# FFN splits, convolution and forms on 1024 columns at once, three of seven products added in PSUM, weight sums from GpSimd to VectorE

## The chip, the cores and the metric

The kernel runs on one core of one Trainium2 chip. The metric is the device time of one execution in microseconds. The core's engines are named as in the profile: PE (TensorE, matrix products), DVE (VectorE), ACT (ScalarE), POOL (GpSimd), and SP (SyncE, which issues the DMAs). SBUF is the core's memory of 128 partitions, PSUM the eight accumulator banks that PE writes; a bank holds 512 fp32 numbers per partition.

## The reference

A decoder trunk in fp32 on one sequence of 1024 tokens and 1024 channels: an mLSTM layer and a convolution (conformer) layer, each followed by a gated feed-forward block with a short convolution, which is what the change is mostly about.

```
def conv_ffn(h, w_up, conv_w, conv_b, w_down):        # h: 1024 tokens x 1024
    u = causal_dwconv(h @ w_up, conv_w, conv_b)       # 1024 x 5632, 3 taps along the tokens
    gate, val = jnp.split(u, 2, axis=-1)              # 2816 each
    return (jax.nn.silu(gate) * val) @ w_down         # 2816 -> 1024

for layer in range(2):
    # six modulation vectors from c (a vector times a 1024 x 6144 matrix, "ada")
    x = x + g1 * mixer(modulate(rmsnorm(x)))          # layer 0 mLSTM (inner width 2048), layer 1 conformer
    x = x + g2 * conv_ffn(modulate(rmsnorm(x)))
return rmsnorm(x)
```

The mLSTM multiplies the normed input by a 1024 x 4096 matrix; the second half of the result is `z`, whose SiLU gates the output.

## The kernel before

Channels lie on the partitions, tokens along the free dimension: 1024 columns (`S`), taken as two halves of 512 (`HS`).

**Products in fp32.** An operand is split into a rounded part and a rest: `split` writes the rounded part with a cast on ACT (L174) and the rest with a subtraction on DVE, or on POOL where `engine` says so (L175). A block of 128 x 128 weights times 512 columns then takes three matmuls (`PASS`).

**Seven products for eight.** In z, in the FFN's up product and in its down product, blocks of the weights and halves of the activations form a 2 x 2 product, which is done with seven multiplications instead of eight. `Forms` prepares the seven left operands from two raw tiles of weights of 128 x 1024 (`raw`, one DMA of 512 KB each): `early` splits a11 and a12, `sums` makes s1, s3, s2 and s4 out of the raw tiles with four additions and subtractions on POOL (L511 to L514), and `late` splits the other five. The right operands b11, b21, t1 to t4, b22 are made once for all pairs. `Seven.product(q)` runs product q: `HALF` = 4 blocks of three matmuls, 12 in all, into a bank of its own; a pair takes 84. The products come in the order 0 to 6.

**The FFN's up product (`ffn_up`).** It loops over 22 pairs j: block j of the gate channels (g) and block j of the value channels (FB + j). Pairs 0 to 2 (`LEAD`) are interleaved with the norm and with the making of the right operands (the start, below); from pair 3 on each pair runs its seven products in turn (the steady pairs). Behind a product its bank is drained into the tiles `u`: `keep` and `tail` copy products 0 and 2 on ACT, and `join` (L633) and `tail` (L718 to L726) make the four results c11, c12, c21, c22 with seven additions on DVE. `conv` makes each half of 512 columns: ACT starts it with a scaled copy (L699), DVE adds two taps (L702). ACT takes the SiLU of the gate's half (L729), POOL multiplies it by the value's half (L730), and SP writes the half to the tensor `p_d` in HBM.

**The passage to the down product.** During the last up pair the operands of the down product are read back from `p_d` (`raw<-p_d`), combined (L573) and split into tiles `h` (L175); the first down step's products 0 to 3 (L807) run as their operands come. `ffn_down` then takes steps m of 84 matmuls; its results are added into x, scaled by the modulation's gate, by `residual` (L457), eight per step.

**z.** The same seven products over eight pairs, with ten blocks of the ada product (L157) on DVE in between; here POOL splits the weights of pairs 2 to 7.

**Order.** A scheduler fixes each engine's order when the kernel is built, from the order and the priorities of the code; on the chip each engine takes its instructions strictly in that order and waits on semaphores. Tiles come out of rings of `bufs` buffers: the tag `wu` has six tiles of 512 columns, `wx` two; a tile is written again when its last reader is done.

Of the kernel before, what the change touches and what calls it, by code (L numbers as in the profile page):

```python
# [79 lines left out]
def trunk(ctx, tc, a):  # L80
# [96 lines left out]
    def load_weight(src, tag="wu", pool=wpool, bufs=6, ahead=30, engine=None, take=None):  # L177
        with tc.high_priority(ahead):
            r = raw_tile()
            n = src.shape[-1] // 2  # L180
            dma(r[:, : 2 * n], src)
            w = []
            for i in range(2):
                t = take() if take else pool.tile([P, 2, 512], F32R, tag=tag, name=nm(tag), bufs=bufs)
# [274 lines left out]
    def ring(*parts):  # L459
        slots = [(pool, tag, n) for pool, tag, n in parts for _ in range(n)]  # L460
        at = [0]

        def take():
            pool, tag, n = slots[at[0] % len(slots)]
            at[0] += 1
            return pool.tile([P, 2, HS], F32R, tag=tag, name=nm(tag), bufs=n)

        return take

    def chain_products(o, w, acts, n, first, last):  # L470
        for k in range(n):
            for q, (i, j) in enumerate(PASS):
# [5 lines left out]
                    stop=last and k == n - 1 and q == 2,  # L478
                )

    class Forms:
        """The seven left operands of the 2 x 2 product with seven multiplications."""

        def __init__(self, g, val, take, engine=None):
            self.src, self.take, self.engine = (g, val), take, engine
            self.raw = [None, None]
            self.rest = None
# [6 lines left out]

        def form(self, name, src):
            t = self.take()
# [10 lines left out]
        def sums(self):  # L507
            a11, a12 = self.load(0)
            a21, a22 = self.load(1)
            s1 = t512()  # L510
            gp.tensor_tensor(s1, a21, a22, ALU.add)  # L511
            gp.tensor_tensor(a21, a11, a21, ALU.subtract)
            gp.tensor_tensor(a11, s1, a11, ALU.subtract)  # L513
            gp.tensor_tensor(a12, a12, a11, ALU.subtract)  # L514
            self.rest = [("s1", s1), ("s3", a21), ("s2", a11), ("s4", a12), ("a22", a22)]

        def late(self, n=5, i=0):
            if self.rest is None:
                self.sums()
            for _ in range(n):  # L520
                self.form(*self.rest.pop(i))

    PRODUCTS = (("a11", "b11"), ("a12", "b21"), ("s1", "t1"), ("s3", "t3"), ("s2", "t2"), ("s4", "b22"), ("a22", "t4"))

    class Seven:
        """C = A B in seven products."""

        def __init__(self, forms, right, n):
            self.forms, self.right, self.n = forms, right, n
            self.banks = [None] * 7  # L530

        def product(self, q):
# [71 lines left out]
    def ffn_up(layer, normed, p_d, hx, ux, es_u, other, ops):  # L604
        first = ring((wpool, "wu", 6))
        pairs = {}

        def pair(j, take):
            pairs[j] = Forms(a["fup"][layer, j], a["fup"][layer, FB + j], take)
            pairs[j].early(j >= LEAD)  # L610
            if 0 < j < 3:
                pairs[j].engine = gp

        LEAD = 3
        for j in range(LEAD):
            pair(j, first)
# [8 lines left out]
        def part(b, h):  # L625
            return u[b][:, FK - 1 + h * HS : FK - 1 + (h + 1) * HS]

        def keep(j, s):
            channel(j)
            sc.copy(part(j, 1), s.banks[0])  # L630
# [1297 lines left out]
```

## Time and profile before

| | |
|---|---|
| median of three runs | 2857.96 us (2856.01 to 2861.04) |
| the profiled execution, first to last instruction | 2862.4 us |
| busy: PE, DVE, ACT, POOL | 2582.8, 2536.0, 1353.0, 1046.6 us |
| granted PE clock over the span | 0.948 of full speed |

The page gives no other time of the profiled execution than its span. By the page's slices the stages are: the mLSTM's up stream to about 290 us; z to 490; attention to 760; the mLSTM's down product to 940; the first FFN's up product to 1400 and its down product to 1600; the conformer to 2130; the second FFN to 2760; the last norm. A busy share is an average over stages with different limits; a busy PE is not PE at its peak, since matmuls are pipelined and their rate follows the granted clock. A row of `windows` gives, for a stretch of time, each engine's busy time with its number of instructions. A row of the timeline gives start, duration and, in brackets, how long the engine had stood idle before it and what released it.

### The profile page before, as it was taken

The page shows a single profiled execution, that of the slowest core. Times are in us where ns is not written, and L with a number is a line of the kernel's source. Part 1 is how long each engine was busy: PE and PEld are TensorE (multiplying, and loading weights), DVE is VectorE, ACT ScalarE, POOL GpSimd, SP SyncE. Part 2 cuts the span into 40 slices and gives each one's busy share as a digit, 9 for nine tenths or more (in the row PEclk, how much of TensorE's full clock was granted, in tenths as well). Part 3 has the DMA queues.
Part 4 walks back from the last instruction along what each step waited for, and adds up shares of the span by engine and source line. Part 5 has one row for each costly group of instructions (what it writes and reads, how often), then busy time and mean ns, then how long its engine had stood idle before and what let it go on. Part 6 is the DMA issues. An engine that isn't in the chain of part 4 may idle for free. (4 is left out here: it accounts for less than half of the span.)

```text
span 2862.4 us, 33276 instructions
## 1 busy us (share of the span) xinstructions
PE 2582.8 (90%) x11405; PEld 2076.4 (73%) x11405; DVE 2536.0 (89%) x3346; ACT 1353.0 (47%) x2422; POOL 1046.6 (37%) x814
## 2 busy tenths in 40 slices
PE   4899798999999899999798998868798999997998
PEld 2788676888788677777576887756576777774777
DVE  7999988777877999999999679996989999999986
ACT  4655334776635444444434342247554444444434
POOL 5312576332100555454432013443225554544220
PEclk7999899999999999999899999988899999997999
DMA  7576357532685222222242331111432222224222
GB/s 264 169 252 221 109 192 239 167 104 67 210 280 185 75 96 74 81 74 82 81 147 94 113 114 46 45 37 31 146 103 67 94 76 81 74 82 151 92 83 94
DMA packets 138392, 342.92 MB, mean 120 GB/s; under 512 B 13872, under 2 KB 36080, under 8 KB 138224
## 3 DMA queue, kind: packets, MB, share of 16 engines
q1 hardware_dynamic: 138224, 340.81, 36.0%
q8 instruction: 90, 1.47, 0.2%
q14 instruction: 78, 0.64, 0.1%
HBM read 264.18 MB, written 73.43 MB: 118 GB/s over the span
## 5 line engine op out<-in xcount | busy, mean ns | idle before, releaser
L473 PE MATMUL ps<-h,wu 128*128 128x512 f32 x4368 | 1065.4, 401 | 71.7 <-DVE wu L175 30.4
L473 PEld LDWEIGHTS ps<-h,wu 128*128 128x128 f32 x4368 | 833.6, 193 | 287.9 <-DVE wu L175 44.6
L195 PE MATMUL ps<-h,wu 128*128 128x512 f32 (+1 forms) x2478 | 585.4, 393 | 17.6 <-DVE h L175 12.0
L195 PEld LDWEIGHTS ps<-h,wu 128*128 128x128 f32 x2478 | 463.1, 191 | 122.2 <-DVE h L175 14.8
L175 DVE TENSOR_TENSOR wu<-raw,wu 128x512 fp32r<-128x512 f32 (+1 forms) x418 | 361.3, 871 | 57.7 <-ACT wu L174 57.1
L702 DVE SCALAR_TENSOR_TENSOR c<-u,par,c 128x512 f32<-128x512 f32 x352 | 374.5, 1091 | 11.9 <-ACT c L699 10.8
L174 ACT CAST wu<-raw 128x512 fp32r<-128x512 f32 (+1 forms) x484 | 288.0, 613 | 188.6 <-PE ps L195 63.9
L511 POOL TENSOR_TENSOR t<-raw 128x512 f32<-128x512 f32 x68 | 108.3, 1593 | 651.1 <-DMA raw<-in_fup 356.6
L699 ACT ACTIVATE c<-u,par 128x512 f32<-128x512 f32 x176 | 138.9, 813 | 372.9 <-DVE u L633 173.0
L473 PE MATMUL ps<-h,wx 128*128 128x512 f32 x1152 | 281.9, 397 | 10.1 <-DVE wx L175 6.7
L473 PEld LDWEIGHTS ps<-h,wx 128*128 128x128 f32 x1152 | 216.2, 188 | 65.7 <-DVE wx L175 10.2
L1680 DVE SCALAR_TENSOR_TENSOR cy<-cu,par,cy 128x512 f32<-128x512 f32 x180 | 179.0, 1031 | 4.6 <-ACT cy L1670 2.7
L730 POOL TENSOR_TENSOR c<-c,c 128x512 f32<-128x512 f32 x88 | 148.5, 1703 | 93.6 <-DVE c L702 88.5
L175 DVE TENSOR_TENSOR h<-raw,h 128x512 fp32r<-128x512 f32 (+1 forms) x204 | 160.7, 817 | 24.2 <-ACT h L174 23.9
L174 ACT CAST h<-raw 128x512 fp32r<-128x512 f32 (+1 forms) x204 | 117.4, 607 | 106.2 <-DVE raw L573 39.9
L157 DVE SCALAR_TENSOR_TENSOR ada<-ada,crep 128x1024 f32<-128x1024 f32 x96 | 126.4, 1320 | 27.0 <-DMA ada<-in_ada 26.8
L175 POOL TENSOR_TENSOR wu<-raw,wu 128x512 fp32r<-128x512 f32 x66 | 107.2, 1640 | 89.3 <-ACT wu L174 89.2
L457 DVE SCALAR_TENSOR_TENSOR x<-ps,mod,x 128x512 f32<-128x512 f32 (+1 forms) x152 | 106.7, 717 | 30.2 <-PE ps L195 23.9
L513 POOL TENSOR_TENSOR raw<-t,raw 128x512 f32<-128x512 f32 x68 | 111.2, 1635 | 36.7 <-DVE wu L175 25.0
L1330 PE MATMUL ps<-q,h 128*128 128x512 f32 (+2 forms) x576 | 117.1, 352 | 1.5 <-ACT q L174 1.3
L1367 PE MATMUL ps<-pt,vr 128*128 128x512 f32 (+2 forms) x576 | 116.2, 351 | 2.4 <-ACT pt L174 1.6
L514 POOL TENSOR_TENSOR raw<-raw 128x512 f32<-128x512 f32 x68 | 111.7, 1643 | 7.8 <-DVE wu L175 3.2
(282 smaller groups left out, 3855.8 us busy)
## 6 DMA issues: line engine op xcount, KB each, us to landing
ada<-in_ada SPq DMA_DIRECT2D x96, 512.0 KB, 4.3
raw<-in_fup SPq DMA_DIRECT2D x94, 512.0 KB, 3.6
p_d<-c SPq DMA_DIRECT2D x88, 256.0 KB, 2.0
raw<-in_pw SPq DMA_DIRECT2D x36, 512.0 KB, 3.6
raw<-in_mup SPq DMA_DIRECT2D x33, 512.0 KB, 4.6
raw<-p_d SPq DMA_DIRECT2D x32, 512.0 KB, 3.3
raw<-in_fdownS SPq DMA_DIRECT2D x32, 512.0 KB, 3.6
raw<-in_mdown SPq DMA_DIRECT2D x24, 512.0 KB, 4.1
```

What stands on the lines that cost most here:

```text
L157: v.scalar_tensor_tensor(w, w, 1.0, crep, ALU.mult, ALU.mult, accum_out=mod[:, layer, b : b + 1])
L174: sc.copy(out_hi, raw)
L175: (engine or v).tensor_tensor(out_lo, raw, out_hi.bitcast(F32), ALU.subtract)
L195: pe.matmul(o, t[:, i, c : c + P], acts[k][:, j, :], start=k == 0 and n == 0, stop=k == nk - 1 and n == 2,)
L473: pe.matmul(o, w[:, i, k * P : (k + 1) * P], acts[k][:, j, :], start=first and k == 0 and q == 0, stop=last and k == n - 1 and q == 2,)
L514: gp.tensor_tensor(a12, a12, a11, ALU.subtract)
L699: sc.activation(c, part(b, h), AF.Identity, scale=taps[FK - 1], bias=pv("fcb", layer, b))
L702: v.scalar_tensor_tensor(c, u[b][:, i + c0 : i + c0 + HS], taps[i], c, ALU.mult, ALU.add)
L730: gp.tensor_tensor(c, s.gates[h], c, ALU.mult)
L1330: pe.matmul(so[:, tlo:], xr[cc][I // nJ][:, i, I % nJ * P : (I % nJ + 1) * P], un["qs"][cc][:, j, tlo:], start=n == 0, stop=n == 3 * CB - 1,)
L1367: pe.matmul(un["num"][cc][:, tlo:], vr[I][:, i, cc * P : (cc + 1) * P], pt[:, j, tlo:], start=I == 0 and n == 0, stop=I == nJ * (hf + 1) - ...
L1680: v.scalar_tensor_tensor(y, u[:, t + c0 : t + c0 + HS], pv("dww", t, j), y, ALU.mult, ALU.add)
```

## The change

- **One instruction for two.** `split` of a raw tile, the FFN's convolution, its SiLU, the gate product and the write of `p_d` work on 1024 columns. Split tiles are `double` tiles of [128, 2, 1024], three in the ring in place of six; s1, which stands alone, gets a single tile (tag `w1`, two buffers, or a slot of the ring of raw tiles).
- **Three products add in PSUM.** Products 1, 5 and 6 accumulate onto the banks of 0, 2 and 3 (`ONTO`), in the order 0, 3, 2, 1, 6, 4, 5. The values of the banks that are overwritten in this way are taken out before: `combine` copies product 0 and product 2 on ACT and adds product 3 on DVE (L573 of the changed kernel). A pair of the up product then has five additions on DVE (L573 to L585) and, with c11, three copies on ACT; a step of the down product has six residuals.
- **From POOL to DVE.** The four sums of a pair (now L522 to L525), the splits of pairs 1 and 2 and of the first down step, and the gate product (now L701). POOL keeps, of this work, the splits of z's pairs 2 to 7, 1024 columns wide.
- The calls of `late` move with it: s1 and raw tile 1 (s3 and a22) are split behind product 6 of the pair before, raw tile 0 (s2 and s4) behind the first product of the pair itself.

DVE in a steady up pair, before: the end of one pair, from the addition of product 5 (L723) on. c are the convolution's tiles, u the results, wu and wx split weights.

```order
L723 TENSOR_TENSOR u_10353<-u_10353,ps_10450 128x512
L175 TENSOR_TENSOR wu_10447<-raw_10377,wu_10447 128x512
L702 SCALAR_TENSOR_TENSOR c_10464<-u_10353,par,c_10464 128x512
L726 TENSOR_TENSOR u_10397<-u_10397,ps_10468 128x512
L702 SCALAR_TENSOR_TENSOR c_10464<-u_10353,par,c_10464 128x512
L175 TENSOR_TENSOR wx_10527<-raw_10525,wx_10527 128x512
L702 SCALAR_TENSOR_TENSOR c_10482<-u_10397,par,c_10482 128x512
L702 SCALAR_TENSOR_TENSOR c_10489<-u_10397,par,c_10489 128x512
L702 SCALAR_TENSOR_TENSOR c_10482<-u_10397,par,c_10482 128x512
L702 SCALAR_TENSOR_TENSOR c_10489<-u_10397,par,c_10489 128x512
L175 TENSOR_TENSOR wx_10530<-raw_10525,wx_10530 128x512
L633 TENSOR_TENSOR u_10509<-u_10509,ps_10512 128x512
```

Products of the pair are drained and its taps follow in halves, up to the next pair's first addition (L633). The same place in the changed kernel, from the addition of product 5 (L585) to the next pair's L573, which empties product 3's bank (w is s1's tile, t its sum):

```order
L585 TENSOR_TENSOR u_8837<-u_8837,ps_8853 128x512
L773 SCALAR_TENSOR_TENSOR c_8929<-u_8866,par,c_8929 128x1024
L175 TENSOR_TENSOR wu_8966<-raw_8883,wu_8966 128x1024
L773 SCALAR_TENSOR_TENSOR c_8929<-u_8866,par,c_8929 128x1024
L773 SCALAR_TENSOR_TENSOR c_8946<-u_8837,par,c_8946 128x1024
L522 TENSOR_TENSOR t_1395_9034<-raw_9020 128x512
L773 SCALAR_TENSOR_TENSOR c_8946<-u_8837,par,c_8946 128x1024
L523 TENSOR_TENSOR raw_9020<-raw_9015,raw_9020 128x512
L175 TENSOR_TENSOR w_1396_9039<-t_1395_9034,w_1396_9039 128x512
L701 TENSOR_TENSOR c_8946<-c_8946,c_8929 128x1024
L573 TENSOR_TENSOR u_8998<-u_8998,ps_8972 128x512
```

The taps (L702, now L773) and the gate product stand together ahead of L573, with the sums between them.

POOL in the passage to the down product, before, from the last up pair's sums on (raw_11511 and raw_11519 are the first down step's weights):

```order
L175 TENSOR_TENSOR wu_11513<-raw_11511,wu_11513 128x512
L511 TENSOR_TENSOR t_1887_11580<-raw_11519 128x512
L512 TENSOR_TENSOR raw_11519<-raw_11511,raw_11519 128x512
L513 TENSOR_TENSOR raw_11511<-t_1887_11580,raw_11511 128x512
L730 TENSOR_TENSOR c_11418<-c_11329,c_11418 128x512
L175 TENSOR_TENSOR wu_11516<-raw_11511,wu_11516 128x512
L514 TENSOR_TENSOR raw_11511<-raw_11511 128x512
L730 TENSOR_TENSOR c_11425<-c_11400,c_11425 128x512
L175 TENSOR_TENSOR wu_11585<-t_1887_11580,wu_11585 128x512
```

and in the changed kernel POOL's last instructions of this FFN and the first of the conformer (L1619):

```order
L675 MEMSET u_10450 128x2
L675 MEMSET u_10553 128x2
L675 MEMSET u_10685 128x2
L675 MEMSET u_10743 128x2
L1619 MEMSET u_1898_12748 128x8x8
```

Sums, splits and gate products have gone to DVE; the zeroing of the two columns ahead of a convolution's tile is left.

PE in a steady up pair, before: products 0 and 1, each four blocks of three matmuls, each with a bank `ps` of its own.

```order
L473 MATMUL ps_8780<-h_7724,wu_8655 128x512 x3
L473 MATMUL ps_8780<-h_7729,wu_8655 128x512 x3
L473 MATMUL ps_8780<-h_7772,wu_8655 128x512 x3
L473 MATMUL ps_8780<-h_7777,wu_8655 128x512 x3
L473 MATMUL ps_8796<-h_7820,wu_8658 128x512 x3
L473 MATMUL ps_8796<-h_7825,wu_8658 128x512 x3
L473 MATMUL ps_8796<-h_7868,wu_8658 128x512 x3
L473 MATMUL ps_8796<-h_7873,wu_8658 128x512 x3
```

And changed: products 2, 1 and 6 of a pair.

```order
L470 MATMUL ps_8721<-h_7891,w_1351_8643 128x512 x3
L470 MATMUL ps_8721<-h_7897,w_1351_8643 128x512 x3
L470 MATMUL ps_8721<-h_7903,w_1351_8643 128x512 x3
L470 MATMUL ps_8721<-h_7909,w_1351_8643 128x512 x3
L470 MATMUL ps_8689<-h_7582,wu_8621 128x512 x3
L470 MATMUL ps_8689<-h_7587,wu_8621 128x512 x3
L470 MATMUL ps_8689<-h_7627,wu_8621 128x512 x3
L470 MATMUL ps_8689<-h_7632,wu_8621 128x512 x3
L470 MATMUL ps_8708<-h_8012,wu_8646 128x512 x3
L470 MATMUL ps_8708<-h_8016,wu_8646 128x512 x3
L470 MATMUL ps_8708<-h_8020,wu_8646 128x512 x3
L470 MATMUL ps_8708<-h_8024,wu_8646 128x512 x3
```

ps_8689 is the bank of product 0 and ps_8708 that of product 3: products 1 and 6 now come behind and add onto them.

The diff, cut to what matters (the calls in z and the start follow the same pattern):

```diff
+    def double(pool=wpool, tag="wu", bufs=3):
+        return pool.tile([P, 2, 2 * HS], F32R, tag=tag, name=nm(tag), bufs=bufs)
...
     class Forms:
+        LATE = ("s1", "raw1", "raw0")
+        def two(self, i, left, right):
+            self.load(i)
+            t = double()
+            split(self.raw[i], t[:, 0], t[:, 1], self.engine)
+            setattr(self, left, t[:, :, :HS])
+            setattr(self, right, t[:, :, HS:])
         def early(self, keep=True):
-            a11, a12 = self.load(0)
-            self.form("a11", a11)
-            self.form("a12", a12)
+            self.two(0, "a11", "a12")
...
-            gp.tensor_tensor(s1, a21, a22, ALU.add)
-            gp.tensor_tensor(a21, a11, a21, ALU.subtract)
-            gp.tensor_tensor(a11, s1, a11, ALU.subtract)
-            gp.tensor_tensor(a12, a12, a11, ALU.subtract)
+            v.tensor_tensor(s1, a21, a22, ALU.add)
+            v.tensor_tensor(a21, a11, a21, ALU.subtract)
+            v.tensor_tensor(a11, s1, a11, ALU.subtract)
+            v.tensor_tensor(a12, a12, a11, ALU.subtract)
...
+    ORDER = (0, 3, 2, 1, 6, 4, 5)
+    ONTO = {1: 0, 5: 2, 6: 3}
     class Seven:
         def product(self, q):
             w, b = PRODUCTS[q]
-            o = self.banks[q] = ps()
-            chain_products(o, getattr(self.forms, w), self.right[b], self.n, True, True)
+            if q in ONTO:
+                self.banks[q] = self.banks[ONTO[q]]
+            else:
+                self.banks[q] = ps()
+            chain_products(self.banks[q], getattr(self.forms, w), self.right[b], self.n, q not in ONTO, True)
+        def combine(self, q, top, bottom, ready):
+            o, done = self.banks, self.done
+            done.add(q)
+            halves = lambda t: (t[:, :HS], t[:, HS:])
+            if q == 0:
+                sc.copy(halves(top())[1], o[0])
+            elif q == 1:
+                ready("c11", o[1])
+            elif q == 2:
+                sc.copy(halves(bottom())[1], o[2])
+            if q in (2, 3) and {2, 3} <= done:
+                c22 = halves(bottom())[1]
+                v.tensor_tensor(c22, c22, o[3], ALU.add)
+            if q == 4:
+                c12, (c21, c22) = halves(top())[1], halves(bottom())
+                self.at = c12 if 6 in done else c21
+                v.tensor_tensor(self.at, c12, o[4], ALU.add)
+                v.tensor_tensor(c22, c22, self.at, ALU.add)
+                ready("c22", c22)
+                if 6 in done:
+                    v.tensor_tensor(c21, c12, o[6], ALU.add)
+                    ready("c21", c21)
+            if (q in (4, 5)) and {4, 5} <= done:
+                c12 = halves(top())[1]
+                v.tensor_tensor(c12, self.at, o[5], ALU.add)
+                ready("c12", c12)
...
     def ffn_up(layer, normed, p_d, hx, ux, es_u, other, ops):
-            if 0 < j < 3:
-                pairs[j].engine = gp
...
+            def ready(name, at):
+                if name == "c11":
+                    sc.copy(top()[:, :HS], at)
+                s.ready.add(name)
+                if name in ("c11", "c12") and {"c11", "c12"} <= s.ready:
+                    s.gate = conv(j)
+                    sc.activation(s.gate, s.gate, AF.Silu)
+                elif name in ("c21", "c22") and {"c21", "c22"} <= s.ready:
+                    s.val = conv(FB + j)
+                if len(s.ready) == 4:
+                    v.tensor_tensor(s.gate, s.gate, s.val, ALU.mult)
+                    dma(p_d[j], s.gate)
...
-            c = rx.tile([P, HS], F32, tag="c", name=nm("c"), bufs=5)
+            c = rx.tile([P, S], F32, tag="c", name=nm("c"), bufs=2)
...
-                    gp.tensor_tensor(c, s.gates[h], c, ALU.mult)
-                    dma(p_d[j][:, h * HS : (h + 1) * HS], c)
...
-                    if q == 2:
-                        down = down_forms(layer, 0, 0, ring((wpool, "wu", 6)), gp)
+                    if q == 1:
+                        down = down_forms(layer, 0, 0, single(wpool, "raw", 3))
```

More of the change, by code (lines that the diff above doesn't have):

```diff
@@ L678, in ffn_up @@
         group(0)
-        pairs[0].late(2)
-        pairs[1].late(1)
+        pairs[0].late("raw1")
+        pairs[1].late("s1")
         group(1)
-        for j, s in enumerate(seven):
-            join(j, s)
         both = seven[:2]
@@ L734, in ffn_up @@
-        for q in range(4, 7):
-            pairs[1].late(1)
-            if q == 6:
-                pairs[2].take = more
-                pairs[2].late()
-            for j, s in enumerate(both):
+        for j, s in enumerate(both):
+            for q in (2, 3):
+                evacuate(j, s, q)
+        pairs[1].one = pairs[2].one = more
+        pairs[1].late("s2", "s4")
+        for j, s in enumerate(both):
+            for q in range(4, 7):
                 s.product(q)
-                if q == 4:
-                    tail(j, s, 2)
-                tail(j, s, q)
+                evacuate(j, s, q)
+                if (j, q) == (1, 5):
+                    pairs[2].late("s1", "raw1")
@@ L744, in ffn_up @@
+        pairs[2].late("raw0")
         for name in ops.FORMS:
@@ L781, in ffn_down @@
             ops.extra, ops.bufs = dx, 1
-            take = ring((dx, "wx", 2), (wpool, "wu", 6))
+            one = single(dx, "w1", 2)
             acts = [[], []]
@@ L816, in ffn_down @@
                         s = Seven(forms, right, CHUNK // 2)
-                    kt = []
-                    for q in range(7):
-                        if m or q > 3:
+                    o = s.banks
+                    for n, q in enumerate(ORDER if m else (0, 1, 2, 3, 6, 4, 5)):
+                        if m or q not in (0, 1, 2, 3):
                             s.product(q)
+                        if not n and m:
+                            forms.late("raw0")
                         if m == KB - 2:
@@ L826, in ffn_down @@
                         if (m + 2, c) != (KB, 1):
-                            if q == 4:
-                                forms = down_forms(layer, c + (m + 2) // KB, (m + 2) % KB, take)
-                            elif q == 5:
-                                forms.late()
-                        elif q == 4:
-                            ws.load(lead)
-                        elif q == 5:
-                            ops.free.sort(key=lambda pool: pool is hpool)
-                            for _ in range(REST):
-                                last(0)
@@ L837, in ffn_down @@
-                        o = s.banks
-                        if q in (0, 2):
-                            kt.append(t512())
-                            sc.copy(kt[-1], o[q])
-                        if q in (0, 1):
-                            residual(o[q], gate(m), m, 0)
-                        elif q == 4:
-                            k1, k5 = kt
+                            if q == 1:
+                                forms = down_forms(layer, c + (m + 2) // KB, (m + 2) % KB, one)
+                            elif q == 6:
+                                forms.late("s1", "raw1")
+                            elif q == 5 and m == KB - 2:
+                                forms.late("raw0")
+                        elif q in (1, 6, 5):
+                            ws.load(1 + (1, 6, 5).index(q))
+                            if q == 5:
+                                ops.free.sort(key=lambda pool: pool is hpool)
+                                for _ in range(REST):
+                                    last(0)
@@ new lines, in ffn_down @@
+                        s.done.add(q)
+                        if q == 0:
+                            k1 = t512()
+                            sc.copy(k1, o[0])
+                            if not m:
+                                residual(o[0], gate(m), m, 0)
+                        elif q == 1:
+                            residual(o[1], gate(m), m, 0)
+                        elif q == 2:
+                            k5 = t512()
+                            sc.copy(k5, o[2])
+                        elif q == 4:
```

305 lines of the change are left out of this document (144 added, 161 removed).

## The prediction

> **What bounds the kernel now.** I read the engines' shares first, then the busy time by stage, then one steady pair of the FFN's up product in time, then who waited for whom. The profiled execution has a span of 2862.4 us, 0.16% above the 2857.96 us median of the three runs; a gain found in the trace is taken off the span and the rest is scaled by that ratio.
>
> ```profile
> PE 2582.8 (90%) x11405; PEld 2076.4 (73%) x11405; DVE 2536.0 (89%) x3346; ACT 1353.0 (47%) x2422; POOL 1046.6 (37%) x814
> ```
>
> ```profile
> core 0: us, PE busy (x) PEld busy (x) DVE busy (x) ACT busy (x) POOL busy (x), PEclk, DMA share, GB/s
> 290.00:490.00 200.00, 175.86 (x709) 138.06 (x707) 175.16 (x266) 74.08 (x127) 134.48 (x86) 0.91 0.52 178
> ...
> 940.00:1078.00 138.00, 125.69 (x511) 98.33 (x509) 134.83 (x149) 66.08 (x110) 74.21 (x56) 0.95 0.23 73
> 1078.00:1400.00 322.00, 307.75 (x1328) 247.97 (x1328) 306.07 (x350) 142.05 (x240) 159.52 (x125) 1.00 0.24 79
> 1400.00:1461.00 61.00, 40.72 (x115) 25.64 (x113) 58.05 (x70) 27.74 (x49) 26.53 (x18) 0.69 0.41 143
> 1461.00:1600.00 139.00, 130.83 (x546) 103.91 (x545) 125.34 (x170) 51.64 (x90) 36.67 (x24) 0.96 0.28 92
> ```
>
> PE and DVE are level at 90% and 89%, so the stages must tell them apart. These rows are z, and then layer 0's FFN: start, steady pairs, passage to the down product, down product. DVE is busy 95 to 98% of the time in the start, the pairs and the passage; in the passage PE's granted clock falls to 0.69. Layer 1 has the same stages at 2130 to 2760 us. A steady pair in time, columns start, duration, engine and line:
>
> ```profile
> 1099.52 16.19 PE L473 MATMUL ps<-h,wu 128*128 128x512 f32 x70 [0.88 <-DVE wu L175]
> 1115.55 3.42 PE L473 MATMUL ps<-h,wx 128*128 128x512 f32 x14
> ...
> 1105.47 0.68 DVE L718 TENSOR_TENSOR u<-u,ps 128x512 f32<-128x512 f32 x1
> 1106.07 0.69 DVE L175 TENSOR_TENSOR wu<-raw,wu 128x512 fp32r<-128x512 f32 x1
> 1106.67 0.68 DVE L719 TENSOR_TENSOR u<-u,ps 128x512 f32<-128x512 f32 x1
> ...
> 1112.67 1.78 DVE L175 TENSOR_TENSOR wx<-raw,wx 128x512 fp32r<-128x512 f32 x1
> 1114.38 3.77 DVE L702 SCALAR_TENSOR_TENSOR c<-u,par,c 128x512 f32<-128x512 f32 x4
> ...
> 1110.48 1.72 POOL L511 TENSOR_TENSOR t<-raw 128x512 f32<-128x512 f32 x1 [8.16 <-DMA raw<-in_fup]
> 1112.28 1.62 POOL L512 TENSOR_TENSOR raw<-raw,raw 128x512 f32<-128x512 f32 x1
> ```
>
> ```profile
> 1098.90:1119.30 20.40, 19.45 (x84) 15.69 (x84) 19.41 (x23) 8.87 (x15) 10.21 (x10) 1.00 0.24 78
> ```
>
> 70 matmuls start within 16.03 us: 0.229 us each. A pair's 84 need 19.24 us, but pairs come every 20.4 us (last row). PE loses 1.15 us per pair, and DVE, busy 19.41 us of 20.4, is what it waits for:
>
> ```profile
> PE ps L473 <- DVE wu L175: 10.5, 12, 0.9
> PE ps L473 <- DVE wx L175: 3.8, 4, 1.0
> ```
>
> ```profile
> PE ps L807 <- DVE h L175: 10.4, 6, 3.4
> PE ps L807 <- ACT h L174: 6.0, 3, 2.8
> ```
>
> The first fence holds the waits in 1078.6 to 1400.8 us, the second those in 1400.8 to 1461.4 us. At 0.229 us per matmul the loss is 138 - 511 x 0.229 = 21 us in the start, 18 in the pairs, 35 in the passage, 14 in the down product and 38 in z. Nearly all that the change can win lies there.
>
> Why DVE is so long: the same split L175 takes 0.69 us at 1106.07, where POOL stands still from 1102.3 to 1110.5 us, and 1.78 us at 1112.67, beside POOL's L512. The prices, first with the shortest, middle and longest of one (ns), then with busy time and mean:
>
> ```profile
> L702 DVE SCALAR_TENSOR_TENSOR c<-u,par,c x352: 735/752/1882, 995.2 to 2618.8; 128x512 f32<-128x512 f32 x176
> ...
> L157 DVE SCALAR_TENSOR_TENSOR ada<-ada,crep x96: 1185/1218/2359, 18.1 to 477.3; 128x1024 f32<-128x1024 f32 x96
> ```
>
> ```profile
> L702 DVE SCALAR_TENSOR_TENSOR c<-u,par,c 128x512 f32<-128x512 f32 x352 | 374.5, 1091 | 11.9 <-ACT c L699 10.8
> L175 DVE TENSOR_TENSOR wu<-raw,wu 128x512 fp32r<-128x512 f32 x406 | 354.7, 881 | 51.7 <-ACT wu L174 51.2
> ...
> L719 DVE TENSOR_TENSOR u<-u,ps 128x512 f32<-128x512 f32 x44 | 29.9, 680 | 0.0
> ...
> L175 DVE TENSOR_TENSOR h<-raw,h 128x384 fp32r<-128x384 f32 x20 | 10.3, 554 | 6.9 <-ACT h L174 6.9
> ...
> L730 POOL TENSOR_TENSOR c<-c,c 128x512 f32<-128x512 f32 x88 | 148.5, 1703 | 93.6 <-DVE c L702 88.5
> ...
> L1776 POOL TENSOR_TENSOR x<-x,gb 128x1024 f32<-128x1024 f32 x8 | 18.7, 2369 | 7.9 <-ACT t L1531 7.9
> ```
>
> L702 and L175 read two operands from SBUF and average 1.09 and 0.88 us against 0.74 and 0.69 alone; L719, which reads one from PSUM, keeps 0.68.
>
> **The change, part by part.** Behind one another, DVE instructions on 512 columns start 0.60 us apart (1105.47, 1106.07, 1106.67), some 0.08 less than they last. From 384 to 512 columns L175 grows by 0.135 us, so a split or product on 1024 should last 0.69 + 4 x 0.135 = 1.23 us, 1.15 from start to start; the 1024-column row that exists (L157) has 1.22, 1.14 to start, and a convolution tap gets 1.17. Two instructions of 512 cost 1.20 to 1.32: a merge saves only 0.05 to 0.15.
>
> *Steady pairs.* Before: 7 splits, 8 taps and 7 adds on DVE; alone these are 14 x 0.60 + 8 x 0.66 = 13.7 us start to start, so 5.7 of the 19.41 us is stretch from POOL's 10.21. After: 3 wide splits and a single one (4.05), 4 wide taps (4.68), 5 adds (3.0), the sums (2.4), the wide gate product (1.15): 15.3 us, 1.6 more than the old list alone. But POOL keeps nothing in the FFN beyond zeroing a two-column edge, so the stretch goes. DVE then needs 15.3 of the 19.24 us that PE needs, and the old wait should fall.
>
> The new wait is product 6 (lines from here on are the changed kernel's). It adds onto product 3's bank, so it must wait until L573 has taken that bank into c22. L573 stands behind, from product 5 of the last pair: L585, a tap, a wide split, two taps, L522, a tap, L523, the single split, the gate product. That is 4 x 0.60 + 4 x 1.17 + 2 x 1.15 = 9.4 us, 10.0 with L573's own 0.60, and up to 0.8 of waiting for ACT's SiLU ahead of the gate product: 10.0 to 10.8. Product 6 is due after four products, 48 x 0.229 = 11.0 us. The slack is 0.2 to 1.0 us, and behind L573 are queued the early split, which the next pair's first product needs some 8 us later, and L577. I leave 0.15 us per pair: 1.0 us over 16 pairs is -16 us per layer; bounds 0 (the wait eats all) and -18.
>
> Costed at nothing: the third ACT copy per pair (under 0.8 us; ACT is busy 8.87 of 20.4); one p_d write of 512 KB for two of 256, whose tile is next written in the next pair, some 9 us later; the load of the weights, issued as early as before. Products 1 and 5 add onto banks that ACT copies two products, 5.5 us, ahead; without that lead a copy's 0.6 us per pair would show.
>
> *Passage.* From the last up pair's start to the end of the first down step DVE sets the pace:
>
> ```profile
> 1380.70:1404.40 23.70, 20.62 (x88) 16.07 (x86) 22.70 (x26) 10.62 (x18) 12.33 (x10) 1.00 0.20 67
> 1404.40:1435.10 30.70, 16.27 (x30) 8.85 (x31) 30.20 (x38) 14.56 (x26) 12.03 (x8) 0.50 0.31 102
> 1435.10:1455.70 20.60, 16.96 (x55) 11.40 (x54) 18.15 (x24) 9.26 (x18) 8.32 (x6) 0.83 0.48 163
> ```
>
> DVE is busy 71 of 75 us. The new order holds 8 wide taps, 7 other wide instructions and 54 on 512 there, the first down step's splits and sums now included: 8 x 1.17 + 7 x 1.15 + 54 x 0.60 = 50 us. The 21 us that this frees is the bound; ACT's waits and the down weights, which now share the ring of raw tiles with s1's split, are late next. I take -13 (bounds -6 and -20).
> Here PE sits at half clock for 30.7 us (0.50 in the second row). The Trainium skill, TensorE: Matmul & The Clock Gate, Part 1, has the array fall to half rate after an idle window of about 3.4 us. The trace agrees in kind: the clock falls behind a wait of 3.4 us. By that rule shorter waits would spare the half rate too and put the passage nearer to -20, the total near 2758 us.
>
> *Start.* DVE takes over the sums of pairs 0 to 2 and POOL's splits of two pairs (7.2 and 8.1 us), less 4 for fewer adds; POOL's 74 us fall away, which at the steady pair's 5.7 us per 10.2 freed 41 of DVE's 135. PE's 117 us would bind. But the order of norm, forms and products still makes PE wait: of 21 us I take -7 (bounds -2 and -12). *Down product.* Two residuals fewer of eight per step, sums added, 37 us of POOL gone: -5 of 14 (bounds -2 and -8).
>
> *z.* Sums go to DVE (4 x 0.60 per pair, 8 pairs), two adds per pair go; POOL keeps the splits of six pairs, in wide pieces of 2.37 us (L1776) for two of 1.70: its work falls from 134 to about 50 us. PE waited for POOL's split once for long:
>
> ```profile
> PE ps L473 <- DVE wu L175: 6.8, 3, 6.1
> PE ps L473 <- POOL wu L175: 5.5, 2, 4.6
> ```
>
> DVE is full of ada blocks there and POOL's late split can come later than two narrow ones did, so I take -4 (bounds +8 and -12).
> The Trainium skill, SBUF — State Buffer, "SBUF: two separate sides", calls the port pair that the two engines share an exclusive lock for a whole instruction. The split at 1112.67 agrees: it ends 0.55 us after POOL's L512. By the rule a wide POOL split holds DVE for up to 2.4 us at a time, yet in all less than before.
>
> *Elsewhere* (up stream, attention, mLSTM's down product, conformer) only pairs of splits merge, 0.05 us each where PE binds: 0, bounds -4 and +3.
>
> **Sum.** (16 + 13 + 7 + 5) x 2 + 4 = 86: span 2776, median 2776.4 x 2857.96 / 2862.4 = 2772 us.
>
> **Rivals.**
> - *Product 6 takes the place of the old wait.* If ACT holds the gate product, L573 comes 1 us late and pairs stay near 20.4 us. For it: slack under 1 us; against: only ACT's wait can use it up. 32 us come back: 2804.
> - *The stages' ends don't gain.* Start, passage and down product wait for ACT, for loads and for each other's order, not for DVE's throughput. For it: the 6.0 us on ACT's L174; against: DVE at 95%. Only the pairs gain, 32 us: 2826.
> - *Slower: the stretch isn't POOL's.* If DMA or ACT traffic stretches those instructions, the wide ones cost twice the means: a tap 2.18, a wide split 1.76. The chain to L573 then grows by 4 x 1.0 + 2 x 0.5 to 15.0 us, pairs take 15.0 + 36 x 0.229 = 23.2 us, +2.8 x 32 = +90: 2948. It decides from a chain of 12.2 us on, where the pair is back at 20.4. Against: 0.69 us at 1106.07 while loads and ACT ran on.
> - *No change.* DVE's 1.6 us more per pair and the waits for banks cancel what the stretch gave: 2858.
> - *All bounds fall well,* as where shorter waits also spare PE the half clock: (18 + 20 + 12 + 8) x 2 + 12 = 128 less: 2730.
>
> **Chances.** Forecast 0.54 (own range 2748 to 2796), product 6 0.15, ends 0.11, all well 0.05, no change 0.05, slower 0.10. The range 2730 to 2834 takes in the forecast, the first two rivals with their scatter and part of the well case, 0.8 in all. Differences under 0.2% (6 us) can't be told from none here: faster 0.85, same 0.05, slower 0.10.
>
> **What would show it.** Right: pairs 19.3 to 19.5 us apart (by the p_d writes), DVE near 16 us busy per pair, taps at 1.2 to 1.3 us, POOL near zero from 940 to 1600 us, PE's waits in the passage under 25 us. Wrong: a wait of PE on L573 in each pair, taps over 1.5 us, or a passage still of 75 us with DVE idle in it. I would be wrong above all if a wait that DVE hid, for a load or ACT, sets the ends.

## The result and the profile after

The changed kernel takes 2764.3 us (median of three runs) against 2859.4 us of the kernel before on the same chip: a ratio of 0.9667, 95% interval 0.9654 to 0.9681, faster by 3.3%. A fourth run, slow at a granted clock of 0.707, took 3348.1 us and is left out; with it the median is 2765.2 us. The forecast was 2772 us, range 2730 to 2834. The profiled execution's span is 2761.8 us, 100.6 under the one before. From the page, the span and the engines' shares:

```profile
span 2761.8 us, 31478 instructions
PE 2545.7 (92%) x11405; PEld 2065.7 (75%) x11405; DVE 2326.3 (84%) x3125; ACT 1323.8 (48%) x2051; POOL 418.3 (15%) x399
```

PE runs the same 11405 matmuls; DVE is busy 210 us less, though it took over work; POOL lost 628 us. The busy time by stage, cut at nearly the same matmuls as the stretches of before (start, pairs, passage, down product of layer 0), and ahead of them z, whose row holds 681 matmuls against 709:

```profile
288.00:481.00 193.00, 165.60 (x681) 128.19 (x680) 170.08 (x277) 74.81 (x111) 77.59 (x40) 0.96 0.56 187
...
925.60:1061.00 135.40, 123.56 (x509) 97.57 (x508) 123.17 (x156) 69.34 (x90) 1.14 (x12) 0.95 0.25 82
1061.00:1364.00 303.00, 303.00 (x1333) 249.75 (x1332) 255.02 (x292) 139.22 (x166) 2.92 (x29) 1.00 0.25 85
1364.00:1407.60 43.60, 32.70 (x112) 23.07 (x111) 40.96 (x59) 21.63 (x32) 0.00 (x0) 0.84 0.50 173
1407.60:1541.70 134.10, 129.01 (x546) 103.50 (x545) 109.63 (x157) 47.16 (x67) 0.00 (x0) 0.97 0.27 90
```

In the pairs PE is busy all of its 303 us and DVE 84% of them. Matched by the number of the matmul, the 100 us come from these places (us):

| place | layer 0 | layer 1 | forecast per layer |
|---|---|---|---|
| start of the up product | -3.3 | -2.1 | -7 |
| steady pairs | -18.9 | -14.3 | -16 |
| passage to the down product | -17.2 | -17.8 | -13 |
| down product | -4.6 | -4.2 | -5 |
| z with attention's first 60 us | -12.0 | | -4 |
| conformer | | -3.9 | 0 |

All else sums to -2. The total was forecast at -86. A steady pair after, from the timeline:

```profile
1118.48 2.66 PE L470 MATMUL ps<-h,wu 128*128 128x512 f32 x11
1120.98 2.96 PE L470 MATMUL ps<-h,w 128*128 128x512 f32 x12
1123.78 14.67 PE L470 MATMUL ps<-h,wu 128*128 128x512 f32 x64
...
1118.68 2.48 DVE L773 SCALAR_TENSOR_TENSOR c<-u,par,c 128x1024 f32<-128x1024 f32 x2
...
1125.23 0.68 DVE L573 TENSOR_TENSOR u<-u,ps 128x512 f32<-128x512 f32 x1
1128.27 1.23 DVE L175 TENSOR_TENSOR wu<-raw,wu 128x1024 fp32r<-128x1024 f32 x1 [2.36 <-ACT wu L174]
...
1134.86 0.69 DVE L585 TENSOR_TENSOR u<-u,ps 128x512 f32<-128x512 f32 x1 [0.71 <-PE ps L470]
```

PE's rows have no brackets: it waits for nothing. Now DVE waits, for ACT and PE, and is busy 255 / 303 x 19.13 = 16.1 us of a pair. Product 1 runs from 1123.78 to 1126.5, then product 6; L573 ends at 1125.91, 0.6 us before. Pairs come 19.13 us apart in layer 0 and 19.43 in layer 1. The prices, from the lines of the trace (shortest, middle, longest in ns) and from the groups by shape (mean):

```profile
L773 DVE SCALAR_TENSOR_TENSOR c<-u,par,c x176: 1274/1280/1287, 978.3 to 2518.4; 128x1024 f32<-128x1024 f32 x176
...
L175 DVE TENSOR_TENSOR wu<-raw,wu x47: 1216/1220/1226, 1060.2 to 1358.5; 128x1024 fp32r<-128x1024 f32 x47
```

The stretch of the taps is gone to the last instruction: 176 taps lie within 13 ns of each other, where the old taps went from 735 to 1882.

### The profile page after: what moved, and what is told of

Its sections match the earlier page's. It is cut to its first block, busy times and chain, and to the rows that moved or that the text cites. A ratio compares the mean times of both kernels' runs of the same rounds, so it can differ in the third digit from the quotient of the medians.

```text
span 2761.8 us, 31478 instructions
## 1 busy us (share of the span) xinstructions
PE 2545.7 (92%) x11405; PEld 2065.7 (75%) x11405; DVE 2326.3 (84%) x3125; ACT 1323.8 (48%) x2051; POOL 418.3 (15%) x399
## 4 chain that ended last, share of the span: by engine, by line
PE 55%; DVE 19%; ACT 4%; issue 3%; DMA 3%; POOL 0%; DVEq 0%; SPq 0%; ACTq 0%; POOLq 0%
PE ps L470 36%; PE ps L203 12%; DVE cy L1726 6%; DVE h L175 3%; PE ps L1376 3%; PE ps L1413 2%; DVE wu L175 2%; DVE raw L628 1%; DMA raw<-p_d 1%; DMA raw<-xc_d 1%; ACT u L1679 1%; PE ps L1358 1%; DVE x L731 1%; DVE c L773 1%; DMA raw<-in_mdown 1%
## 5 line engine op out<-in xcount | busy, mean ns | idle before, releaser
L470 PE MATMUL ps<-h,wu 128*128 128x512 f32 x4704 | 1122.7, 397 | 37.5 <-DVE zv L573 11.2
L470 PEld LDWEIGHTS ps<-h,wu 128*128 128x128 f32 x4704 | 892.9, 191 | 254.1 <-DVE zv L573 13.7
L174 ACT CAST wu<-raw 128x1024 fp32r<-128x1024 f32 (+1 forms) x282 | 294.1, 1044 | 257.6 <-PE ps L470 99.8
L175 DVE TENSOR_TENSOR wu<-raw,wu 128x1024 fp32r<-128x1024 f32 (+1 forms) x262 | 320.2, 1223 | 110.5 <-ACT wu L174 109.7
L773 DVE SCALAR_TENSOR_TENSOR c<-u,par,c 128x1024 f32<-128x1024 f32 x176 | 221.2, 1280 | 1.0 <-ACT c L771 1.0
L771 ACT ACTIVATE c<-u,par 128x1024 f32<-128x1024 f32 x88 | 108.9, 1243 | 139.7 <-DVE u L581 138.3
L470 PE MATMUL ps<-h,w 128*128 128x512 f32 x672 | 166.3, 395 | 0.0
L174 ACT CAST h<-raw 128x512 fp32r<-128x512 f32 (+1 forms) x204 | 116.8, 607 | 93.8 <-DVE raw L628 43.0
L175 DVE TENSOR_TENSOR h<-raw,h 128x512 fp32r<-128x512 f32 (+1 forms) x204 | 135.6, 695 | 19.3 <-ACT h L174 19.1
L470 PEld LDWEIGHTS ps<-h,w 128*128 128x128 f32 x672 | 126.1, 188 | 30.1 <-ACT u L570 0.6
L1376 PEld LDWEIGHTS ps<-q,h 128*128 128x128 f32 x576 | 94.4, 188 | 17.1 <-ACT t L1441 2.0
L203 PE MATMUL ps<-go,wu 128*128 128x512 f32 x384 | 87.8, 390 | 0.0
L203 PE MATMUL ps<-h,h 128*128 128x512 f32 (+1 forms) x450 | 83.8, 347 | 0.0
L203 PEld LDWEIGHTS ps<-go,wu 128*128 128x128 f32 x384 | 72.1, 188 | 15.4 <-issue 0.5
L174 ACT CAST w<-t 128x512 fp32r<-128x512 f32 x54 | 33.5, 621 | 101.2 <-DVE t L522 101.2
```

The lines of the kernel that those rows point to most:

```text
L174: sc.copy(out_hi, raw)
L175: (engine or v).tensor_tensor(out_lo, raw, out_hi.bitcast(F32), ALU.subtract)
L203: pe.matmul(o, t[:, i, c : c + P], acts[k][:, j, :], start=k == 0 and n == 0, stop=k == nk - 1 and n == 2,)
L470: pe.matmul(o, w[:, i, k * P : (k + 1) * P], acts[k][:, j, :], start=first and k == 0 and q == 0, stop=last and k == n - 1 and q == 2, ski ...
L771: sc.activation(c, body(b), AF.Identity, scale=taps[FK - 1], bias=pv("fcb", layer, b))
L773: v.scalar_tensor_tensor(c, u[b][:, i : i + S], taps[i], c, ALU.mult, ALU.add)
```

## The experiments

Theory P: POOL's work beside DVE stretched DVE's instructions, and that set the pace of the FFN. Rival W: DVE's load in instructions set it, so merges and adds in PSUM brought the gain. Rival L: the sums came late from POOL. Each ratio is to the kernel before, timed beside the run. Times by stage compare the profiled executions, matched by the number of the matmul.

**One part of the change alone: the sums on DVE.** In the kernel before:

```diff
-            gp.tensor_tensor(s1, a21, a22, ALU.add)
+            v.tensor_tensor(s1, a21, a22, ALU.add)
```
and the three behind it likewise.

> The kernel before with one part of the change alone: the four weight sums of a pair run on VectorE instead of GpSimd; gate product, splits and widths as before. Theory P (GpSimd stretches VectorE's instructions, 0.56 us per us of its own work, and that sets the pace): VectorE gets 2.4 us more work per up pair, 16.1 us alone, but GpSimd keeps only 3.4 us per pair, so 1.9 us of stretch: 18.0 us, under TensorE's 19.2; pairs 19.3 to 19.7 us apart instead of 20.4, total 2800 to 2830 us. Rival W (VectorE's load in instructions sets the pace, and the merges and the adds in PSUM carried the gain): 2.4 us on top of 19.4 in each pair, pairs near 21.8 us, total about 2900 us.

2762.6 us, ratio 0.9665 (0.9649 to 0.9681): four lines of code give what the whole change gives. It lies beyond P's range on P's side, and W is out by 140 us. The pairs, by stage:

```profile
1057.90:1361.70 303.80, 303.80 (x1332) 249.71 (x1331) 294.21 (x420) 149.24 (x244) 71.42 (x64) 1.00 0.26 86
```

PE is busy throughout although DVE still has 294 of 303.8 us and POOL keeps the gate product. The passages came with it (-19 us each); my range had not counted them.

**Everything of the FFN off POOL, nothing merged.** Sums as above, and

```diff
-                    gp.tensor_tensor(c, s.gates[h], c, ALU.mult)
+                    v.tensor_tensor(c, s.gates[h], c, ALU.mult)
```
with the splits of pairs 1 and 2 and of the first down step on DVE.

> The kernel before with everything of the FFN taken off GpSimd (sums, splits of pairs 1 and 2 and of the first down step, gate product) and nothing merged or added in PSUM: all instructions stay at 512 columns, seven banks per pair. Theory P: VectorE has 13.7 + 2.4 + 1.2 = 17.3 us per up pair and no stretch, pairs 19.2 to 19.5 us apart; most of the change's 94 us is there, total 2775 to 2800 us. Rival W: 3.6 us more instructions per pair on the engine that sets the pace, pairs near 23 us, total about 2940 us.

2755.1 us, ratio 0.9637 (0.9623 to 0.9652), 9 us under the changed kernel, and below P's range. DVE has 442 instructions in 296 us of the pairs, where the changed kernel has 292 in 303, and the steady pairs come 19.1 us apart all the same:

```profile
1064.00:1360.00 296.00, 296.00 (x1298) 243.22 (x1297) 279.73 (x442) 146.41 (x239) 2.72 (x27) 1.00 0.26 85
```

**The adds in PSUM undone in the up product.** `ONTO` is empty for its `Seven`, each product has a bank, and `combine` makes seven additions:

```diff
-            if q in ONTO:
-                self.banks[q] = self.banks[ONTO[q]]
+            if q in self.onto:
+                self.banks[q] = self.banks[self.onto[q]]
```

> The changed kernel with the up product's seven products in a bank each again and seven additions on VectorE (z and the down product keep the adds in PSUM). Theory P: 1.2 us more per pair, 16.5 us, stays under TensorE's 19.2, and the wait of product 6 goes: 2758 to 2775 us. Rival W (the adds saved in PSUM carry a part of the gain): 1.2 us per pair, 40 pairs: 2800 to 2815 us.

2756.2 us, ratio 0.9644 (0.9624 to 0.9663): 8 us under the changed kernel, 2 us under P's range and far from W. The intervals of the two ratios just overlap, so the times alone don't settle these 8 us. The traces place them. The pairs keep 19.13 and 19.43 us; the two starts give it: -7.2 against -0.3 us in the first 95 us of layer 0's, -5.6 against +1.6 in the first 48 us of layer 1's. Each later run with separate banks in the up product and no work added on POOL shows the same, -6.5 to -7.5 and -4.2 to -5.7 us. PE's waits in the first 95 us of layer 0's start, in the changed kernel (two rows) and in this run:

```profile
PE ps L470 <- ACT h L174: 8.0, 4, 4.4
PE ps L470 <- ACT u L570: 1.8, 1, 1.8
```

```profile
PE ps L470 <- ACT h L174: 4.9, 3, 1.9
```

The wait for the copy L570 of product 2's bank is gone, and PE waits 3.1 us less for ACT's casts of the operands; why the casts come earlier wasn't followed up.

**The sums back on POOL in the changed kernel.**

```diff
-            v.tensor_tensor(s1, a21, a22, ALU.add)
+            gp.tensor_tensor(s1, a21, a22, ALU.add)
```

> The changed kernel with the four sums of a pair back on GpSimd. Theory P: GpSimd's 6.6 us per pair stretch VectorE by up to 3.7 us while it loses 2.4 us of work: 16.6 us, still under TensorE's 19.2, so the pairs stay within 0.3 us of 19.2; the passages and starts, where VectorE has no room, get longer: total 2770 to 2795 us. Rival W (fewer instructions on VectorE are better): 2750 to 2765 us.

2877.4 us, ratio 1.0066 (1.0046 to 1.0086): 0.7% over the kernel before, the whole gain lost, and outside both expectations. I had looked at DVE's sum (16.6 us of 19.2) and not at the chain to L573. The timeline of a pair:

```profile
1251.74 2.39 DVE L773 SCALAR_TENSOR_TENSOR c<-u,par,c 128x1024 f32<-128x1024 f32 x1
1254.05 2.31 DVE L175 TENSOR_TENSOR wu<-raw,wu 128x1024 fp32r<-128x1024 f32 x1
...
1261.67 1.23 DVE L701 TENSOR_TENSOR c<-c,c 128x1024 f32<-128x1024 f32 x1 [1.13 <-ACT c L697]
1262.82 0.68 DVE L573 TENSOR_TENSOR u<-u,ps 128x512 f32<-128x512 f32 x1
...
1263.55 0.73 PE L470 MATMUL ps<-h,wu 128*128 128x512 f32 x2 [1.49 <-DVE u L573]
```

One tap and one split take twice their 1.28 and 1.22 us beside POOL's L522 and L523, 2.2 us more together. The two sums are off DVE, 1.2 us less, but that is not won: they had filled the time of ACT's SiLU (L697), and now the gate product L701 waits 1.13 us for it. From product 5's end at 1251.1 to L573's end the chain has 12.4 us, against 10.2 in the changed kernel; 12.4 + 36 x 0.229 = 20.6 us, and the pairs came 20.8 to 21.0 apart. This is the first rival of the prediction, with its cause, ACT holding the gate product, as one part and POOL's stretch as the other. Against the changed kernel the pairs lose 48 us, the starts 27, the down products 17, z 13 and the passages 5.

**POOL work whose result nobody reads.** In the changed kernel, when c12 is ready:

```diff
+                if name == "c12":
+                    for _ in range(4):
+                        gp.tensor_tensor(idle, at, at, ALU.mult)
```

> The changed kernel with GpSimd work that nothing waits for: in each up pair four products of 512 columns that read c12 twice and write a tile that nobody reads, started when c12 is ready, so beside the taps ahead of L573. No other instruction moves. It tells contention from delay: in the kernel before, the sums on GpSimd also come late by their own 6.6 us, and that alone could have made TensorE wait. Theory P (contention): 0.37 to 0.56 us of stretch per us of GpSimd, 2.4 to 3.7 us on the chain to L573, of which 0.5 us is slack; product 6 waits 1.9 to 3.2 us in each of some 36 pairs, pairs 21.0 to 22.4 us apart, total 2830 to 2880 us. Rival L (the sums' delay was the cost, GpSimd's traffic costs nothing): pairs stay at 19.1 to 19.4, total 2763 to 2768 us.

2937.1 us, ratio 1.0263 (1.0248 to 1.0278): L is out, and it is worse than P expected. (ACT waits for this POOL work ten times, 3.9 us in all, before it writes over c12.) In time, the POOL work, three DVE stretches and PE:

```profile
1243.67 8.03 POOL L697 TENSOR_TENSOR idle<-u 128x512 f32<-128x512 f32 x4 [13.63 <-DVE u L585]
...
1244.78 2.06 DVE L175 TENSOR_TENSOR wu<-raw,wu 128x1024 fp32r<-128x1024 f32 x1
1246.76 4.04 DVE L777 SCALAR_TENSOR_TENSOR c<-u,par,c 128x1024 f32<-128x1024 f32 x2
1250.72 1.52 DVE L522 TENSOR_TENSOR t<-raw 128x512 f32<-128x512 f32 x1
...
1256.44 5.76 PE L470 MATMUL ps<-h,wu 128*128 128x512 f32 x17 [2.61 <-DVE u L573]
```

The stretch is 0.84 + 1.56 + 0.83 = 3.2 us for 8.03 us of POOL, as forecast, and the wait of product 6 is 2.6 us, as forecast. But most pairs come 23.66 us apart, where the chain gives 13.4 + 36 x 0.229 = 21.6: behind the wait PE meets the half clock, by the busy time in two stretches of the pair before. The third row is a later pair, from one wait's end to the next, that doesn't meet it:

```profile
1232.80:1237.30 4.50, 4.50 (x13) 3.62 (x14) 2.61 (x3) 0.00 (x0) 0.00 (x0) 0.64 0.31 120
1237.30:1256.40 19.10, 16.53 (x72) 13.24 (x71) 16.69 (x15) 8.51 (x10) 7.93 (x6) 1.00 0.17 55
...
1279.90:1301.90 22.00, 19.42 (x84) 15.69 (x84) 19.27 (x19) 8.50 (x11) 7.94 (x6) 1.00 0.21 72
```

In the first 4.5 us the clock is 0.64 and 13 matmuls start; 4.5 / 0.229 would be 20. That is 4.5 - 13 x 0.229 = 1.5 us lost. The pair at full clock took 22.04 us after the same wait, so the half clock costs 23.66 - 22.04 = 1.6 of the missing 2.0 us. Of the 29 such waits between 1090 and 1436 us and between 2320 and 2655 us, 25 meet the half clock, for 3.41 us each, and four do not.

**The same POOL work with a bank for each product** (the up product as in the run without adds in PSUM).

> The same idle GpSimd work (four products of 512 columns per up pair) in the changed kernel with a bank for each product of the up product (2756.2 us). VectorE: 16.5 us and 3.2 us of stretch, 19.7 us against TensorE's 19.2. If the 172 us that this work cost the changed kernel came through product 6, which waits for L573 and then meets the half clock, only about 0.5 us per pair is left here: 2770 to 2790 us. If VectorE's lost time itself was the cost, without the shared bank: 2850 us and more.

2818.5 us, ratio 0.9852 (0.9837 to 0.9866), between the two expectations. The pairs are 20.09 us apart with waits of 0.6 to 0.7 us, and DVE is busy 277 of the 280 us from 1100 to 1380:

```profile
1207.38 6.45 POOL L725 TENSOR_TENSOR idle<-u 128x512 f32<-128x512 f32 x4 [9.88 <-DVE u L586]
...
1210.87 6.43 DVE L805 SCALAR_TENSOR_TENSOR c<-u,par,c 128x1024 f32<-128x1024 f32 x4
...
1221.45 2.83 PE L470 MATMUL ps<-h,wu 128*128 128x512 f32 x11 [0.62 <-DVE wu L175]
```

My 16.5 us of DVE per pair were too few (278 us in 302.9 without the load are 17.6); the rest came in the passages, which gained 5 and 7 us instead of 16 each, and in the starts, 17 us. So, by the comparison of these two kernels, of the changed kernel's 4.5 us per pair DVE's lost time itself costs 1.0 and the shared bank with the half clock 3.6.

**The same load in the old layout**, with the sums early on DVE:

```diff
                 s.gates.append(conv(g, 1))
+                for _ in range(4):
+                    gp.tensor_tensor(g0[:, : HS - 4], g1[:, : HS - 4], g1[:, : HS - 4], ALU.mult)
```

> The kernel before with the FFN's work taken off GpSimd (2755.1 us), and GpSimd given work that nothing waits for: four products of 508 columns in each up pair, started when the gate's taps have read their tile. The sums stay on VectorE and come early. It asks in the old layout, with a bank for each product, whether GpSimd's traffic or the sums' delay made the old pairs 20.4 us. Theory P: VectorE is busy 18.1 us per pair; 0.40 us of stretch per us of GpSimd's 6.6 to 8 us gives 20.7 to 21.3 us, pairs 20.3 to 21.5 us apart, total 2800 to 2840 us. Rival L (delay): pairs stay under 19.5, total 2753 to 2762 us.

2830.3 us, ratio 0.9894 (0.9879 to 0.9909), in P's range; L alone is out here too. (ACT waits for this POOL work twice, 7.1 us of the 75 that it costs.) POOL works 5.7 us a pair, pairs are 20.3 us apart, and PE waits as in the kernel before, for the same two splits (1090 to 1380 us):

```profile
PE ps L473 <- DVE wu L175: 5.9, 9, 0.8
PE ps L473 <- DVE wx L175: 2.9, 4, 0.9
```

So POOL's work is enough to hold the old pairs back without any delay of the sums. That the delay cost nothing on top, in the kernel before, isn't shown.

**z.** In the changed kernel PE waits there for product 3's bank, the rival again in another place. The waits of 288 to 481 us, then three rows of the timeline:

```profile
PE ps L470 <- DVE zv L573: 11.2, 6, 3.3
PE ps L470 <- ACT zg L566: 4.7, 3, 3.0
```

```profile
426.40 1.23 DVE L157 SCALAR_TENSOR_TENSOR ada<-ada,crep 128x1024 f32<-128x1024 f32 x1 [1.66 <-DMA ada<-in_ada]
...
427.55 0.68 DVE L573 TENSOR_TENSOR zv<-zv,ps 128x512 f32<-128x512 f32 x1
...
428.29 3.98 PE L470 MATMUL ps<-h,wu 128*128 128x512 f32 x16 [1.60 <-DVE zv L573]
```

L573 itself waited for nothing; it stood behind an ada block that waited for its DMA. Two of the six waits are of this kind (1.6 and 1.9 us). The longest, 3.3 us, stands behind splits of h, one of which waited 2.6 us for ACT, so the expectations below make more of the ada blocks than the trace bears out. Three attempts to take the wait away: a bank for each product in z; product 6 last; and banks in both places. In the first and third, pair 0 of z takes c12 through the SiLU before product 4's terms are added, so they don't compute the reference and stand here for their time alone.

> The changed kernel with z's seven products in a bank each and seven additions per pair on VectorE; the FFN as changed. Theory P: in z product 6 waits for L573, which stands on VectorE behind ada blocks that wait for their DMA (11.2 us of waits in the trace, six times); without the shared bank that goes, and attention starts 5 to 12 us earlier: 2752 to 2760 us. Rival (the ada blocks' DMA paces z anyway, the wait only moves to another product): 2762 to 2768 us.

> The changed kernel with z's pairs 2 to 7 in the order 0, 3, 2, 1, 4, 5, 6, all adds in PSUM kept: product 6 comes two products, 5.5 us, later and L573 has that much more time. Theory P: the six waits of 11.2 us in all fall under 3 us, total 2753 to 2761 us. Rival (s2, split on GpSimd behind product 0, is now needed one product earlier and takes the wait over): 2763 to 2770 us.

> The changed kernel with a bank for each product in the up product and in z (the down product keeps its adds in PSUM): the run without adds in PSUM in the up product took 2756.2 us, 9 us under the changed kernel; if z gives its 5 to 12 us on top, 2744 to 2752 us. Rival: z's gain is taken back by attention's start, 2755 to 2758 us.

2767.4, 2772.6 and 2759.6 us: no gain, a loss of 8 us, and 3 us more than the up product's banks alone; none reached its first expectation. With product 6 last the wait moved to POOL's wide splits (288 to 487 us):

```profile
PE ps L470 <- POOL wu L175: 10.4, 5, 3.3
```

With separate banks in z the last of z's matmuls come 8 us earlier than in the changed kernel (first and third attempt), and attention's first 60 us take 8 to 11 us longer. A fourth, with the products of a11 and a12 first so that their wide tile comes free early, and a fifth, with narrow splits again:

> A version that takes what the runs showed: the changed kernel with a bank for each product in the up product and in z, and in z's pairs 2 to 7 the order 0, 1, 3, 6, 2, 4, 5, so that the wide tile of a11 and a12 comes free two products earlier and the next weights' splits on GpSimd start earlier. The theory that z is held by its three wide tiles and the late splits expects 2744 to 2752 us; the rival (z goes by the ada blocks' DMA) 2754 to 2762 us.

> The changed kernel with a bank for each product in the up product (2756.2 us), and z's splits on GpSimd in two pieces of 512 columns again, with their casts; the tiles stay wide. In z both kernels with narrow splits reached product 4 of pair 5 at 428.5 to 429.6 us, the changed one at 442.7. If a wide split on GpSimd (2.4 us, and its 1.05 us cast ahead of it) is what comes late there, 2745 to 2752 us; if it is the ring of three wide tiles that lets a split start late, whatever its width, 2754 to 2759 us.

2760.7 us (ratio 0.9645, 0.9629 to 0.9661) and 2755.8 us (0.9633, 0.9612 to 0.9653), against 2756.2 without these edits, both in the range of the second expectation: neither the order nor the width alone holds z. The two runs with the old z code had gained 21 us by attention's first 60 us, the changed kernel 14. What costs it those 7 us stays open; that the old z has six small tiles and makes five late splits a product or two earlier is argued, not shown: a fourth wide tile wasn't tried.

The fastest versions are the kernel before with its FFN off POOL (2755.1) and the changed one with separate banks in the up product (2756.2, 2755.8), the same within their intervals and 8 to 9 us under the change.

## Why the prediction was right, point by point

- *What bounds the kernel* held: DVE, stretched by POOL, set the FFN's pace. The slower rival, that the stretch isn't POOL's, is refuted by the taps of 1274 to 1287 ns, while DMA (85 GB/s in the pairs, 79 before) and ACT went on.
- *Prices* held: a wide split 1.22 us (1.23 forecast), a wide tap 1.20 from start to start (1.17), POOL's wide split in z 2.41 in the median (2.37).
- *Steady pairs* held in size: 19.13 us against 19.24 + 0.15. The chain to L573 took 10.2 us (10.0 to 10.8), the slack 0.6 (0.2 to 1.0). Layer 1's pairs take 0.3 us more, without a wait: its matmuls start 231 ns apart where layer 0's start 227.
- *The credit* went partly to the wrong edits. My sum of 15.3 us counted merges and saved adds as if DVE's load alone mattered; with them DVE has 3 us of a pair to spare (255 of 303 us busy), without them still 1 (280 of 296). The runs show the move of the sums worth 96 us, the rest of the FFN's move 7; the merges and adds in PSUM together cost 9, or 1, which is within the noise, where the up product's banks stay separate.
- *Passage* mis-sized: -17.5, not -13, so the second rival, that the ends don't gain, is out. I took it near the middle of its bounds for fear of ACT and the ring; DVE's 41 of 43.6 us shows it still bound by DVE. PE's longest waits there (8.7 us) end on ACT's cast L174 of h, and that cast waits for DVE (7.7 us on L628). By the rule that the prediction takes from the Trainium skill (TensorE: Matmul & The Clock Gate, Part 1) the passage would come near -20; the half clock there fell from 37.6 to 13.7 us in all, so the trace agrees in direction. It does not agree on the 3.4 us. Before, the clock had fallen 1.5 us into the wait that ends at 1406.0, not behind it as the prediction reads:

```profile
1402.60:1404.10 1.50, 0.04 (x1) 0.00 (x0) 1.50 (x2) 0.01 (x1) 1.50 (x2) 1.00 0.00 0
1404.20:1406.00 1.80, 0.00 (x1) 0.01 (x1) 1.80 (x3) 0.00 (x0) 1.80 (x2) 0.50 0.00 0
```

  (PEclk is the third figure from the right.) And with the POOL work whose result nobody reads, it fell behind waits of 2.5 to 2.6 us, so a shorter idle time was enough here.
- *Start* mis-sized the other way: -2.7 in the mean, not -7. PE's order waits stayed, 8.0 us for ACT's casts in the first 95 us of layer 0's alone, and the shared banks added their own: with separate banks the starts gain 9 us each.
- *z and attention* gave -12 instead of -4, and still less than the sums alone (-20). POOL's work in z fell from 134 to 78 us, not to about 50: the sum left out the operands h and the small products ms, 22 us, which stay on POOL.
- *The total* came within 8 us in part by luck: the starts fell 9 us short of their 14, and that hid a part of what the passages (9 us), z with attention (8) and the conformer (4) gained beyond the forecast.
- *The first rival* did not come in the pairs, by 0.6 us, but waits on L573 came in z, 11.2 us, and, as soon as POOL worked again, in the pairs.
- *What stretches.* The prediction shows L719, which reads PSUM, keeping 0.68 us; but in layer 0's steady pairs POOL stands still beside it. L726, another such addition, runs wholly beside POOL in each of these pairs and keeps its time too, where a split does not:

```profile
L726 DVE TENSOR_TENSOR u<-u,ps x16: 675/682/684, 1090.6 to 1396.1; 128x512 f32<-128x512 f32 x16
...
L175 DVE TENSOR_TENSOR wu<-raw,wu x71: 680/687/1784, 1077.3 to 1390.0; 128x512 fp32r<-128x512 f32 x71
```

- The Trainium skill, SBUF — State Buffer, calls the shared port pair an exclusive lock for a whole instruction ("SBUF: two separate sides"). The trace agrees that the additions that read PSUM don't stretch (0.68 us). Whether the loser blocks for a whole instruction stays open: beside the taps of the changed kernel a POOL product took 2.0 us, the shortest of its kind 1.04, and the split and taps next to it 2.0 to 2.1 for 1.2 to 1.3. Both engines wait, about as if they took turns.

## What to carry to other kernels

Before counting instructions on a busy engine, look at the longest and the shortest time of the same instruction: if they differ by two, find what runs beside the long ones, and move that first. Work put on an idle engine isn't free where it shares a path with the one that sets the pace. A resource shared to save work (a bank) turns slack into a deadline: compute the chain to it, not the sum, and ask what a small slip costs once PE's clock falls.

## What the runs showed of the hardware that I had not expected

- Waits of 1.3 to 1.5 us in each pair left PE's clock full (pairs of 20.8 to 21.0 us); of waits of 2.5 to 2.6 us 25 in 29 met 3.41 us of half clock, 1.6 us on top of the pair. In a row of such pairs the half clock begins every 23.89 us, seven times 3.41, and the waits end every 23.66; it slides from about the wait's end to 1.5 us behind it, and then one pair goes without.
- POOL is stretched as well: its four products took 8.03 us beside the changed kernel's taps, and 6.45 beside the other order; the shortest single one took 1.04 us, so four would take 4.2.
- Matmuls of the same shape start 227 to 236 ns apart with no wait between them, by their place in the pair and alike in each pair: in layer 0 only product 2, whose weights lie in the tile w, takes 232 to 235 ns, in layer 1 most products take 231 to 236. Whether the place of the weights or of the other operand makes it isn't shown.
